# Retention's squares and roots moved by a round, one-column sums in another form, and norm-weight scaling moved by a supertile, in a two-layer encoder trunk

## The chip, the cores and the metric

One core of one Trainium2 chip runs the kernel. The metric is device time in microseconds (us) from the start to the end of one execution. The kernel before the change was timed three times: 2040.69, 2045.63 and 2047.82 us, median 2045.63 us. A further execution was profiled.

## What is computed

Two layers act on x, 2048 tokens of 1024 columns, and a final RMSNorm ends the work:

```
hn   = rms_norm(x, norm_gain)
proj = hn @ w_in                      # 1024 -> 8 sections of 512 columns
ya   = chunked_rel_attention(aq, ak, av, rel_bias)   # 8 heads x 64, own chunk and 8 left
yr   = rms_norm(o_intra + o_inter)    # 4 retention heads x 128, chunkwise recurrent
x    = x + concat(ya * silu(ag), yr * silu(rg)) @ w_out
```

In the retention part, o_intra multiplies decayed scores (q times k, times a decay mask) with v; o_inter multiplies q with a running state; the state is scaled and added to, chunk after chunk. The sum o is divided, per row and head, by the root of its mean square.

## The kernel before

**Number format.** Each projection and most other products are made of three float16 matmuls: a value is split in an upper half and the rest (upper times upper, upper times rest, rest times upper). The ScalarE (ACT) usually writes the upper half by a copy; the VectorE (DVE) then writes the rest.

**Loops.** Layer l has four column groups s (two attention heads and one retention head each), and each group runs over four supertiles n of 512 tokens. For each (l, s, n), `dense_T` computes q, k and the rotary q and k (line 763: 4 x 24 matmuls of 128x512), and `dense_V` computes the two v and the two gates (line 783: 4 x 24). While these run, the attention and retention of the *previous* supertile run between their matmuls. After the four groups, `wout` (line 1161) multiplies with w_out and adds to x, row tile by row tile; the last group's attention and retention run beside its first rounds. In the first layer the second layer's input norm and first weights are prepared beside it as well.

**Rounds.** Everything goes by rounds. `run` advances the dense generator by one step (8 matmuls of 128x512), calls `tick`, which issues what was put off with `later(k, fn)` and is due in this round, in the order in which it was put off, then advances the attention by one step, and last pulls steps of the background list `bg` (weights of the next group, `prep_T`, `prep_V`, `prep_Omax`, `prep_O`). A supertile has 12 rounds of `dense_T` and 12 of `dense_V`.

**Order of the queues.** TensorE (PE), ACT, DVE and GpSimd (POOL) stand under a manual schedule: each executes its instructions in the order in which the Python code issues them. An instruction that waits holds all behind it on its engine. SyncE (SP) issues the DMAs; its order is made by a planner from the program, save for DMAs that `in_turn` keeps in program order.

**An attention unit** (one head, 128 queries, three rounds): scores S on PE (lines 831, 832); bias and row maximum on DVE (L835, L837); the exponential on ACT (L838) and its float16 copy (L840); the rest on POOL (L841); a DMA transposes both (L843, tile pT); three rounds later PE multiplies with v (L853, L854).

**A retention tile** (128 tokens, tile a of the supertile):

| round | instructions |
|---|---|
| 6a | scores r1 on PE (L888) |
| 6a+1 | decay mask, DVE L907 |
| 6a+2 | upper half dT, ACT L892 |
| 6a+3 | rest of dT, DVE L896 |
| 6a+5 | output and state products r2, PE L888; the last of the output's six products reads the rest of dT |
| +1 | state addition, DVE L928 |
| +2 | upper half of the state (sh), ACT L892; square of the output with a row sum into ss, ACT L949 |
| +3 | rest of the state, DVE L896; `root`: mean and epsilon on DVE L940, power -1/2 on POOL L941 |
| +4 | `fin`: output times root times gate, DVE L945; its store goes out a round later (L947) |
| +5 | state times the chunk decay, ACT L936 |

The rounds marked +k count from the round of r2. The next tile's round 6a+6 is +1, so its mask (L907) is issued at +2, its upper half at +3 and its rest (L896, dT) at +4, where `fin` of the tile before stands ahead of it.

**One-column work.** Each weight section is scaled by a power of two. `sumsq` squares it on ACT (L320) with a row sum, `lowp` casts the column (L327), `allsum` sums over the rows by a matmul with ones (L334), and `norm_scale` makes the scales on DVE (L151 to L155). `prep_Omax` does the same for w_out over eight blocks and adds their columns one by one (L522); its matmul (msO) follows four rounds after the last addition, and six one-column instructions (L336 to L531) follow that. `gain_scale(1)` does a like chain for the second layer's norm weights in three parts; it is started at (l, s, n) = (0, 1, 1), beside `prep_T` of the next group.

Of the kernel before, what the change touches and what calls it, by code (L numbers as in the profile page):

```python
# [10 lines left out]
F32 = mybir.dt.float32  # L11
I32 = mybir.dt.int32
AF = mybir.ActivationFunctionType
ALU = mybir.AluOpType
# [4 lines left out]
P = 128  # L19
# [8 lines left out]
def hybrid_trunk(ctx: ExitStack, tc: tile.TileContext, x, pos, gain, gcol, w_in, w_out, rel, fgain,  # L28
# [8 lines left out]
    act, dve, pool, pe, sp = nc.scalar, nc.vector, nc.gpsimd, nc.tensor, nc.sync  # L37
# [24 lines left out]
    mhalf = cp.tile([P, 1], F32, tag="mhalf", name="mhalf")  # L62
# [83 lines left out]
    def norm_scale(sq, nm, ig=None, k=14):  # L146

        e = b2.tile([P, 1], I32, tag="p2e", name=f"e{nm}")
        s = b2.tile([P, 1], I32, tag="p2s", name=f"s{nm}", bufs=8)
        i = b2.tile([P, 1], I32, tag="p2i", name=f"i{nm}", bufs=12)  # L150
        dve.tensor_scalar(e, sq.bitcast(I32), 24, 23, op0=ALU.logical_shift_right, op1=ALU.logical_shift_left)  # L151
        dve.tensor_scalar(s, e, -1.0, float((190 + k) << 23), op0=ALU.mult, op1=ALU.add)
        dve.tensor_scalar(i, e, float((64 - k) << 23), None, op0=ALU.add)
        if ig is not None:
            dve.tensor_tensor(i.bitcast(F32), i.bitcast(F32), ig, op=ALU.mult)  # L155
        return s.bitcast(F32), i.bitcast(F32)

    gains = {}
# [249 lines left out]
    def V_units(l, s, g, iv, nm):  # L408

        g.urv = mul_cols("urv", dcs[:, s:s + 1], None, 2.0 ** -11, nm)  # L410
        g.ugh = mul_cols("ugh", iv[2], None, 2.0 ** -11, nm)
        g.ka = mul_cols("ka", iv[0], iv[2], 2.0 ** -5, nm)
        gk = mul_cols("gqk", iv[2], dcs[:, 4 + s:5 + s], 2.0 ** -11, nm)
        g.re = mul_cols("re", iv[1], g.qk, 2.0 ** (31 + s), nm)
        act.activation(g.re, g.re, AF.Copy, scale=gk[:, 0:1])
        yield
        for u in (gk, g.re):
            dve.tensor_tensor(u, u, u, op=ALU.mult)
            dve.reciprocal(u, u)
        dve.tensor_scalar(g.re, g.re, EPS, 2.0 ** -120, op0=ALU.mult, op1=ALU.max)  # L420
        dve.tensor_scalar(g.re, g.re, 2.0 ** 120, None, op0=ALU.min)
        g.ra = mul_cols("ra", gk, dcs[:, 8 + s:9 + s], 1.0, nm)
        yield

    def prep_V(l, s, g):
        nm = f"V{l}_{s}"
        g.vh = b3.tile([P, KT, 512], F16, tag="wh", name=f"wh{nm}")
        g.vl = b3.tile([P, KT, 512], F16, tag="wl", name=f"wl{nm}")
        c0 = s * P
        sts = []  # L430

        def ld(j):
            o = VSEC[j] * 512 + c0
            sts.append(load_sec(w_in[l, :, o:o + P], f"{nm}{j}"))

        def sq(j):
            return sumsq(sts[j], f"{nm}{j}", g.vh[:, :, j * P:(j + 1) * P])

        def cv(j, s_):
            return convert(sts[j], g.vh[:, :, j * P:(j + 1) * P], g.vl[:, :, j * P:(j + 1) * P], s_)  # L440

        def rest(k):
            for _ in range(k):
                yield

        ld(0)
        ld(1)
        yield
        iv = [None] * 3
        m1 = [None] * 2  # L450
        for j in range(2):
            yield
            m1[j] = lowp(sq(j), f"{nm}{j}")
            yield from rest(3)
            m = allsum(m1[j], f"{nm}{j}")
            sv, iv[j] = norm_scale(m, f"{nm}{j}", gains[l].i)
            yield from cv(j, sv)
            ld(2 + j)
        yield from rest(1)
        m2 = sq(2)  # L460
        yield
        yield from rest(1)
        m3 = sq(3)
        dve.tensor_tensor(m2, m2, m3, op=ALU.add)
        m2 = lowp(m2, f"{nm}2")
        yield
        yield from rest(2)
        m = allsum(m2, f"{nm}2")
        sv, iv[2] = norm_scale(m, f"{nm}2", gains[l].i)
        for _ in V_units(l, s, g, iv, nm):  # L470
            pass
        yield from cv(2, sv)
        yield from cv(3, sv)
        g.vdone = 4

    def prep_V_next(l, g):

        nm = f"V{l}_0"
        src = [w_in[l, :, VSEC[j] * 512:VSEC[j] * 512 + P] for j in range(4)]
        sts = [load_sec(src[j], f"{nm}{j}", True) for j in range(2)]  # L480
        yield
        for j in (2, 3):
            st = b2.tile([P, KT, P], F32, tag="q", name=f"st{nm}{j}")
            sp.dma_start(st, src[j].rearrange("(k p) c -> p k c", p=P))
            sts.append([(st, 0, KT)])
        yield
        g.vh = b3.tile([P, KT, 512], F16, tag="wh", name=f"wh{nm}")
        g.vl = b3.tile([P, KT, 512], F16, tag="wl", name=f"wl{nm}")
        hi, lo = ([w_[:, :, j * P:(j + 1) * P] for j in range(4)] for w_ in (g.vh, g.vl))
        m = [lowp(sumsq(sts[j], f"{nm}{j}", hi[j]), f"{nm}{j}") for j in range(2)]  # L490
        yield
        m2, m3 = (sumsq(sts[j], f"{nm}{j}", hi[j]) for j in (2, 3))
        dve.tensor_tensor(m2, m2, m3, op=ALU.add)
        m.append(lowp(m2, f"{nm}2"))
        yield
        yield
        iv = [None] * 3
        for j in (2, 0, 1):
            sv, iv[j] = norm_scale(allsum(m[j], f"{nm}{j}"), f"{nm}{j}", gains[l].i)
            for i in ((2, 3) if j == 2 else (j,)):  # L500
                yield from convert(sts[i], hi[i], lo[i], sv)
        yield from V_units(l, 0, g, iv, nm)
        g.vdone = 4

    def prep_Omax(l, go):
        nm = f"O{l}"
        mm = b2.tile([P, 1], F32, tag="omax", name=f"omax{nm}")
        load = lambda j: load_sec(w_out[l, :, j * P:(j + 1) * P], f"{nm}m{j}")
        for _ in range(4):
            yield  # L510
        sts = [load(0), load(1)]
        for _ in range(4):
            yield
        for j in range(KT):
            yield
            m1 = sumsq(sts[j], f"{nm}m{j}", None)
            if j + 2 < KT:
                sts.append(load(j + 2))
            if j == 0:
                dve.tensor_copy(mm, m1)  # L520
            else:
                dve.tensor_tensor(mm, mm, m1, op=ALU.add)  # L522
        mm = lowp(mm, nm)
        for _ in range(4):
            yield
        m = allsum(mm, nm)
        sv, iv = norm_scale(m, nm)
        go.os = b2.tile([P, 1], F32, tag="o_s", name=f"o_s{l}")
        go.oi = b2.tile([P, 1], F32, tag="o_i", name=f"o_i{l}")
        dve.tensor_copy(go.os, sv)  # L530
        dve.tensor_copy(go.oi, iv)  # L531
        yield
# [87 lines left out]
    def later(k, fn):  # L620
        deferred.append([k, fn])
# [276 lines left out]
    def retention(l, s, n, g, st):  # L898
        for a in range(4):
# [18 lines left out]
            if not last:  # L918
# [4 lines left out]
                ns = ring["state"]  # L923
# [9 lines left out]
                later(1, add)  # L933
                later(2, lambda sh=sh, ns=ns: upper_of(sh, ns))
                later(3, lambda sh=sh, ns=ns: rest_of(sh, ns))
                later(5, lambda ns=ns: act.activation(ns, ns, AF.Copy, scale=(1.0 - 2.0 ** (-5 - s)) ** P))  # L936
            ss = b2.tile([P, 1], F32, tag="rss", name=f"rss{nm}")

            def root(ss=ss):
                dve.tensor_scalar(ss, ss, g.ra[:, 0:1], g.re[:, 0:1], op0=ALU.mult, op1=ALU.add)  # L940
                pool.tensor_tensor(ss, ss, mhalf, op=ALU.pow)  # L941

            def fin(t=t, a=a, r2=r2, ss=ss, nm=nm):
                y = b1.tile([P, P], F32, tag="yr", name=f"yr{nm}")
# [1 line left out]
                                         op0=ALU.mult, op1=ALU.mult)  # L946
                later(1, lambda: in_turn(sp.dma_start(y_d[t][:, 512 + s * P:512 + (s + 1) * P], y)))  # L947

            later(2, lambda r2=r2, ss=ss: act.activation(r2[:, 2 * P:3 * P], r2[:, 0:P], AF.Square,  # L949
                                                         accum_out=ss))  # L950
            later(3, root)
            later(4, fin)
            yield


# [32 lines left out]
    def y_scale(u, go):  # L988
        dve.tensor_scalar(u.m, u.m, 2.0 ** -100, None, op0=ALU.max)
        u.sy, iy = norm_scale(u.m, u.nm)  # L990
        u.sc = b2.tile([P, 1], F32, tag="osc", name=f"osc{u.nm}", bufs=4)
        dve.tensor_tensor(u.sc, iy, go.oi, op=ALU.mult)

    def y_turn(u):
        if u.t + 1 == NT:
# [262 lines left out]
    def weight_steps():  # L1258
# [20 lines left out]
        def vsq(j):  # L1279
            m[j] = sumsq(sts[j], f"{nm}{j}", g.vh[:, :, j * P:(j + 1) * P])  # L1280
            if j == 3:
                dve.tensor_tensor(m[2], m[2], m[3], op=ALU.add)
            if j != 2:
                m[j] = lowp(m[min(j, 2)], f"{nm}{j}")

# [186 lines left out]
    for l in range(DEPTH):  # L1472
        gO = [Grp(), Grp()]
        go = Grp()
        for s in range(NSW):
            g = grp(l, s)
            for n in range(NS):
# [12 lines left out]
                if (l, s) == (0, 0) and 0 < n < NS - 1:  # L1490
# [3 lines left out]
                    if n == 2:  # L1494
                        t3 = tables((3,), [xs0[3][:, i * 256:(i + 1) * 256] for i in range(4)])
                        steps["v"] = lambda: go_on(t3)
                if (l, s, n) == (0, 1, 1):
                    for l_ in range(1, DEPTH):
                        gr = gain_scale(l_)
                        later(2, lambda gr=gr: next(gr))  # L1500
                        later(10, lambda gr=gr: next(gr))
                        later(18, lambda gr=gr: next(gr))
# [113 lines left out]
```

## Time and profile before

| | |
|---|---|
| median of three runs | 2045.63 us |
| the profiled execution, its own time | 2046.1 us |
| its span, first to last instruction | 2044.0 us |
| mean granted TensorE clock | 0.995 |
| PE, DVE, ACT, POOL busy | 1992.2, 1249.5, 1136.1, 694.1 us |
| DMA | 313.47 MB, 153 GB/s on average |

The span and the execution's own time differ by 2.1 us, which lies around the instructions. Engines overlap, so that their busy times don't add up. A line of the view of waits names the instruction that sat waiting, what released it, the total in us, how often and the longest. In the timeline a row has its start in us from the span's start, its duration in us, engine, line, operation and tiles, and in brackets the idle time of the engine ahead of it with the releaser.

### The profile page before, as it was taken

How to read it: one execution, taken by the hardware profiler on the slowest of the kernel's cores; microseconds unless marked ns; L12 is line 12 of the kernel's file. 1: busy time of each engine (PE TensorE's matmuls, PEld its weight loads, DVE VectorE, ACT ScalarE, POOL GpSimd, SP SyncE). 2: the span in 40 equal slices, each digit the busy share in tenths (PEclk: the TensorE clock that was granted, in tenths of full speed). 3: DMA queues.
4: the chain of work that ended last, by engine and by line, in shares of the span. 5: the costliest groups of instructions: out<-in, count | busy, mean ns of one | idle time of the engine just before them, and what ended most of it. 6: DMA issues, size and time to landing. Idle time of an engine off the chain costs nothing. (4 is left out here: it accounts for less than half of the span.)

```text
span 2044.0 us, 36842 instructions
## 1 busy us (share of the span) xinstructions
PE 1992.2 (97%) x12918; PEld 1047.1 (51%) x12918; DVE 1249.5 (61%) x3676; ACT 1136.1 (56%) x2526; POOL 694.1 (34%) x701
## 2 busy tenths in 40 slices
PE   7998999999999999999999999999999999999998
PEld 5444554555545555554444555555555555555444
DVE  7687766565666555676553656565656566557543
ACT  7565765465565654655444546655656565455432
POOL 1344433443334434430003433444343434343100
PEclk9999999999999999999999999999999999999999
DMA  8787775456575654899774647454656766558874
GB/s 234 180 180 161 162 147 116 107 129 146 118 177 126 162 131 101 170 215 262 216 188 110 129 100 162 113 130 99 160 120 146 156 156 127 123 120 187 227 204 136
DMA packets 645690, 313.47 MB, mean 153 GB/s; under 512 B 459232, under 2 KB 602080, under 8 KB 645504
## 3 DMA queue, kind: packets, MB, share of 16 engines
q1 hardware_dynamic: 645504, 311.12, 65.3%
q8 instruction: 101, 1.65, 0.3%
q14 instruction: 85, 0.70, 0.1%
HBM read 123.26 MB, written 41.98 MB: 81 GB/s over the span
## 5 line engine op out<-in xcount | busy, mean ns | idle before, releaser
L841 POOL TENSOR_TENSOR pq<-sc,pq 128x640 f16<-128x640 f32 (+4 forms) x256 | 322.0, 1258 | 857.6 <-ACT pq L840 460.5
L838 ACT ACTIVATE sc<-sc,mq,cT 128x640 f32<-128x640 f32 (+4 forms) x256 | 218.4, 853 | 597.0 <-DVE mq L837 432.3
L783 PE MATMUL dV<-whV,hTh 128*128 128x512 f16 x1024 | 352.0, 379 | 1.3 <-DVE gt L801 1.3
L763 PE MATMUL dT<-hTh,whT 128*128 128x512 f16 x1008 | 348.5, 381 | 4.0 <-DVE xa L94 3.9
L783 PE MATMUL dV<-wlV,hTh 128*128 128x512 f16 x1024 | 352.0, 379 | 0.0
L783 PE MATMUL dV<-whV,hTl 128*128 128x512 f16 x1024 | 351.8, 379 | 0.0
L763 PE MATMUL dT<-hTh,wlT 128*128 128x512 f16 x1008 | 347.8, 380 | 0.0
L763 PE MATMUL dT<-hTl,whT 128*128 128x512 f16 x1008 | 346.9, 379 | 0.0
L783 PEld LDWEIGHTS <-hTh 128*128 128x128 f16 x2048 | 196.3, 98 | 214.8 <-DVE gt L801 2.7
L763 PEld LDWEIGHTS <-whT 128*128 128x128 f16 x2016 | 192.6, 98 | 210.6 <-DVE xa L94 4.4
L835 DVE CUSTOM_DVE_ANT_0 sc<-S,bias 128x640 f32<-128x640 f32 (+4 forms) x256 | 188.4, 736 | 91.6 <-PE S L832 89.6
L1161 PE MATMUL dO<-whO,yhy 128*128 128x512 f16 x504 | 191.8, 381 | 1.8 <-DMA yhy<-hTh 1.8
L1161 PE MATMUL dO<-whO,yly 128*128 128x512 f16 x504 | 191.7, 380 | 0.3 <-DMA yly<-hTh 0.3
L1161 PE MATMUL dO<-wlO,yhy 128*128 128x512 f16 x504 | 191.6, 380 | 0.0
L840 ACT ACTIVATE pq<-sc 128x640 f16<-128x640 f32 (+4 forms) x256 | 171.5, 670 | 8.1
L1161 PEld LDWEIGHTS <-yhy 128*128 128x128 f16 x1008 | 98.3, 98 | 115.5 <-DMA yhy<-hTh 2.3
L783 PEld LDWEIGHTS <-hTl 128*128 128x128 f16 x1024 | 99.1, 98 | 111.7 <-issue 2.1
L763 PEld LDWEIGHTS <-wlT 128*128 128x128 f16 x1008 | 97.7, 98 | 108.8 <-issue 1.5
L853 PE MATMUL o<-v,pT 128*128 128x129 f16 x1120 | 133.1, 222 | 14.7 <-DMA pT<-pq 14.6
L831 PE MATMUL S<-k,q 128*128 128x128 f16 (+3 forms) x592 | 143.1, 268 | 0.0
L832 PE MATMUL S<-k,q 128*128 128x128 f16 (+3 forms) x592 | 130.0, 268 | 0.0
L853 PEld LDWEIGHTS <-pT 128*128 128x128 f16 x1120 | 103.5, 98 | 50.7 <-DMA pT<-pq 22.6
(360 smaller groups left out, 3283.3 us busy)
## 6 DMA issues: line engine op xcount, KB each, us to landing
q<-qq SPq DMA_DIRECT2D x128, 128.0 KB, 2.4
yyy<-y_d SPq DMA_DIRECT2D x32, 512.0 KB, 4.5
stT<-in_w_in_dram SPq DMA_DIRECT2D x27, 512.0 KB, 4.9
stV<-in_w_in_dram SPq DMA_DIRECT2D x26, 512.0 KB, 4.5
k<-kk SPq DMA_DIRECT2D x128, 64.0 KB, 2.0
swp<-rot SPq DMA_DIRECT2D x64, 128.0 KB, 3.0
tabc<-tab SPq DMA_DIRECT2D x32, 256.0 KB, 2.9
tabs<-tab SPq DMA_DIRECT2D x32, 256.0 KB, 3.1
```

Of the source, the lines that this page charges most:

```text
L763: pe.matmul(ps, w_[:, j, kt, :], h_[:, kt, :], start=(m == 0), stop=(m == 23))
L783: pe.matmul(ps, h_[:, kt, a * P:(a + 1) * P], w_[:, kt, :], start=(m == 0), stop=(m == 23))
L831: pe.matmul(o, st.q[:, hx, 0, cs], k_, start=True, stop=False)
L832: pe.matmul(o, st.q[:, hx, 1, cs], k_, start=False, stop=True)
L835: dve.tensor_tensor_reduce(out=v, in0=S[:, 0:w], in1=g.bias[hx][:, 640 - w:640], scale=1.0, scalar=-3.0e38, op0=ALU.add, op1=ALU.max, accu ...
L838: act.activation(v, v, AF.Exp, bias=m[:, 0:1], scale=g.c[:, 0:1])
L840: act.activation(pq[:, 0:w], v, AF.Copy)
L841: pool.tensor_tensor(pq[:, w:2 * w], v, pq[:, 0:w], op=ALU.subtract)
L853: pe.matmul(o[:, u.hx, 0:129], u.p[:, b, :], v_, start=(b == 0), stop=False)
L1161: pe.matmul(ps, h_[:, kt, :], w_[:, kt, :], start=(m == 0), stop=(m == 23))
```

## The change

- Retention: the square is issued at +1 instead of +2, the root at +2 instead of +3, the state's decay at +4 instead of +5. `fin` is still due at +4, but it is put off from inside `root`, so that it is now issued behind the next tile's rest of dT of that round.
- Seven places of one-column products and sums on DVE change from tensor_tensor to tensor_scalar with the second column as a per-row scalar.
- `prep_Omax` waits five rounds instead of four ahead of its matmul.
- `gain_scale(1)` starts at (0, 1, 2) instead of (0, 1, 1).

```diff
-            dve.tensor_tensor(i.bitcast(F32), i.bitcast(F32), ig, op=ALU.mult)
+            dve.tensor_scalar(i.bitcast(F32), i.bitcast(F32), ig[:, 0:1], None, op0=ALU.mult)
...
-            dve.tensor_tensor(u, u, u, op=ALU.mult)
+            dve.tensor_scalar(u, u, u[:, 0:1], None, op0=ALU.mult)
...
-        dve.tensor_tensor(m2, m2, m3, op=ALU.add)
+        dve.tensor_scalar(m2, m2, 1.0, m3[:, 0:1], op0=ALU.mult, op1=ALU.add)
...
-                dve.tensor_tensor(mm, mm, m1, op=ALU.add)
+                dve.tensor_scalar(mm, mm, 1.0, m1[:, 0:1], op0=ALU.mult, op1=ALU.add)
         mm = lowp(mm, nm)
-        for _ in range(4):
+        for _ in range(5):
             yield
...
-                later(5, lambda ns=ns: act.activation(ns, ns, AF.Copy, scale=(1.0 - 2.0 ** (-5 - s)) ** P))
+                later(4, lambda ns=ns: act.activation(ns, ns, AF.Copy, scale=(1.0 - 2.0 ** (-5 - s)) ** P))
...
+            def root(ss=ss, fin=fin):
+                dve.tensor_scalar(ss, ss, g.ra[:, 0:1], g.re[:, 0:1], op0=ALU.mult, op1=ALU.add)
+                pool.tensor_tensor(ss, ss, mhalf, op=ALU.pow)
+                later(2, fin)
+
-            later(2, lambda r2=r2, ss=ss: act.activation(r2[:, 2 * P:3 * P], r2[:, 0:P], AF.Square,
+            later(1, lambda r2=r2, ss=ss: act.activation(r2[:, 2 * P:3 * P], r2[:, 0:P], AF.Square,
                                                          accum_out=ss))
-            later(3, root)
-            later(4, fin)
+            later(2, root)
...
-        dve.tensor_tensor(u.sc, iy, go.oi, op=ALU.mult)
+        dve.tensor_scalar(u.sc, iy, go.oi[:, 0:1], None, op0=ALU.mult)
...
-                if (l, s, n) == (0, 1, 1):
+                if (l, s, n) == (0, 1, 2):
                     for l_ in range(1, DEPTH):
                         gr = gain_scale(l_)
```

The additions in `prep_V_next` and in `vsq` change like the one in `prep_V` that is shown. In the built programs PE's matmuls keep their order except for four one-column ones (msg, msh and the two msO), which move later. On SP ten or so of the DMAs change places with a neighbour, mostly a pT transpose that now stands ahead of a store or of the transpose of rotary k. On POOL the root's power keeps its place among the exponentials' rests (L841) but for the first of all; it moves ahead of the bias memsets (L597, L598) in six places and ahead of the row norms' powers (L219) in eight.

More of the change, by code (lines that the diff above doesn't have):

```diff
@@ L492, in prep_V_next @@
         m2, m3 = (sumsq(sts[j], f"{nm}{j}", hi[j]) for j in (2, 3))
-        dve.tensor_tensor(m2, m2, m3, op=ALU.add)
+        dve.tensor_scalar(m2, m2, 1.0, m3[:, 0:1], op0=ALU.mult, op1=ALU.add)
         m.append(lowp(m2, f"{nm}2"))
@@ L935, in retention @@
                 later(3, lambda sh=sh, ns=ns: rest_of(sh, ns))
-                later(5, lambda ns=ns: act.activation(ns, ns, AF.Copy, scale=(1.0 - 2.0 ** (-5 - s)) ** P))
+                later(4, lambda ns=ns: act.activation(ns, ns, AF.Copy, scale=(1.0 - 2.0 ** (-5 - s)) ** P))
             ss = b2.tile([P, 1], F32, tag="rss", name=f"rss{nm}")
-            def root(ss=ss):
-                dve.tensor_scalar(ss, ss, g.ra[:, 0:1], g.re[:, 0:1], op0=ALU.mult, op1=ALU.add)
-                pool.tensor_tensor(ss, ss, mhalf, op=ALU.pow)
             def fin(t=t, a=a, r2=r2, ss=ss, nm=nm):
@@ L1281, in vsq @@
             if j == 3:
-                dve.tensor_tensor(m[2], m[2], m[3], op=ALU.add)
+                dve.tensor_scalar(m[2], m[2], 1.0, m[3][:, 0:1], op0=ALU.mult, op1=ALU.add)
             if j != 2:
```

## The prediction

> **What bounds the kernel now.** I read the page's busy times first, then what PE waited for.
>
> ```profile
> PE 1992.2 (97%) x12918; PEld 1047.1 (51%) x12918; DVE 1249.5 (61%) x3676; ACT 1136.1 (56%) x2526; POOL 694.1 (34%) x701
> ```
>
> PE works for 1992.2 of the span's 2044.0 us and the change leaves its work as it is. Only the 51.8 us without a matmul can shrink, and a new wait on another engine costs nothing until PE meets it. So the view of waits, for PE alone, is the ledger (line waited, releaser, total us, times, longest):
>
> ```profile
> PE o L853 <- DMA pT<-pq: 14.6, 12, 2.7
> PE r L888 <- DVE dT L896: 6.5, 7, 1.6
> PE dO L1161 <- DMA yhy<-hTh: 1.8, 1, 1.8
> PE dV L783 <- DVE gt L801: 1.3, 2, 0.7
> PE msT L334 <- DVE mbT L327: 1.2, 1, 1.2
> PE msO L334 <- DVE mbO L327: 0.2, 1, 0.2
> ```
>
> The first line, DMA transposes of the softmax, is the largest, and no edit acts on it directly. The lines released by DVE, 9.2 us together, are an in-order engine being late, and the change works on its queue and on those that feed it. The timeline of PE gives their places (start, duration, idle ahead):
>
> ```profile
> 339.42 0.16 PE L334 MATMUL msT<-mbT,ones 128*128 128x1 bf16 x1 [1.23 <-DVE mbT L327]
> ...
> 586.98 0.23 PE L888 MATMUL r<-rv,dT 128*128 128x128 f16 x1 [1.32 <-DVE dT L896]
> ...
> 594.64 0.39 PE L783 MATMUL dV<-whV,hTh 128*128 128x512 f16 x1 [0.64 <-DVE gt L801]
> ...
> 601.99 0.23 PE L888 MATMUL r<-rv,dT 128*128 128x128 f16 x1 [0.67 <-DVE dT L896]
> ...
> 860.01 0.23 PE L888 MATMUL r<-rv,dT 128*128 128x128 f16 x1 [1.60 <-DVE dT L896]
> 862.96 0.23 PE L853 MATMUL o<-v,pT 128*128 128x129 f16 x1 [0.83 <-DMA pT<-pq]
> ...
> 1594.51 0.39 PE L783 MATMUL dV<-whV,hTh 128*128 128x512 f16 x1 [0.66 <-DVE gt L801]
> ...
> 1601.85 0.23 PE L888 MATMUL r<-rv,dT 128*128 128x128 f16 x1 [0.67 <-DVE dT L896]
> ```
>
> So the waits stand where one-column chains run: beside the norm weights (339), the w_out sums of both layers (587 to 602, and 1594, 1602), and where w_out is multiplied first (860). Elsewhere DVE and ACT are late without PE noticing.
>
> **The change, part by part.**
>
> *Norm weights one supertile on.* The timeline of DVE ahead of 339:
>
> ```profile
> 329.56 0.15 DVE L336 TENSOR_SCALAR m2h<-msh 128x1 f32<-128x1 f32 x1
> ...
> 332.02 0.15 DVE L196 SCALAR_TENSOR_TENSOR ge<-gi 128x1 f32<-128x1 f32 x1
> ...
> 339.21 0.16 DVE L327 CAST mbT<-m1T 128x1 bf16<-128x1 f32 x1 [3.44 <-ACT whT L320]
> ```
>
> The norm-weight chain holds DVE from 329.56 to 332.17, 2.6 us. Behind it come the row maximum, the exponential that waits for it, and only then on ACT the weight square that feeds mbT. With the chain gone all of these come up to 2.6 us sooner, more than the 1.23 us that PE waits: **-1.2 us**. The chain now runs in the next supertile (two windows, one a supertile: length, busy times PE, PEld, DVE, ACT, POOL):
>
> ```profile
> 313.00:365.00 52.00, 50.60 (x329) 26.09 (x327) 35.85 (x121) 28.97 (x71) 19.69 (x19) 1.00 0.52 114
> 365.00:417.00 52.00, 52.00 (x366) 28.26 (x365) 28.42 (x85) 25.19 (x59) 20.95 (x19) 1.00 0.50 116
> ```
>
> There PE never idles and DVE has 23.6 us free of 52, because no weights are prepared. I cost the chain at nothing there; without that cover it would cost its 2.6 us once, since the row maximum and the gate's rest, which free PSUM, queue behind it.
>
> *The w_out sums: tensor_scalar, and a round more.* The timeline of DVE around 587 to 602:
>
> ```profile
> 586.29 0.16 DVE L522 TENSOR_TENSOR omaxO<-omaxO,m1O0m 128x1 f32<-128x1 f32 x1 [0.44 <-ACT stO0m L320]
> 586.38 0.35 DVE L945 SCALAR_TENSOR_TENSOR yr<-r,rss,gt 128x128 f32<-128x128 f32 x1
> 586.65 0.28 DVE L896 SCALAR_TENSOR_TENSOR dT<-dT,r 128x128 f16<-128x128 f16 x1
> ...
> 592.47 1.12 DVE L522 TENSOR_TENSOR omaxO<-omaxO,m1O0m 128x1 f32<-128x1 f32 x1
> ...
> 600.67 0.15 DVE L336 TENSOR_SCALAR m2O<-msO 128x1 f32<-128x1 f32 x1
> ...
> 601.38 0.35 DVE L945 SCALAR_TENSOR_TENSOR yr<-r,rss,gt 128x128 f32<-128x128 f32 x1
> 601.65 0.28 DVE L896 SCALAR_TENSOR_TENSOR dT<-dT,r 128x128 f16<-128x128 f16 x1
> ```
>
> One sum of one column takes 0.16 us or 1.12 us. The view by line gives the spread (min/median/max in ns), beside forms that use per-row scalars already:
>
> ```profile
> L155 DVE TENSOR_TENSOR iT<-iT,gi x28: 159/161/1326, 199.5 to 1549.8; 128x1 f32<-128x1 f32 x28
> L992 DVE TENSOR_TENSOR oscy<-iy,o_i x32: 158/160/162, 816.9 to 2014.0; 128x1 f32<-128x1 f32 x32
> L837 DVE TENSOR_SCALAR mq<-mq,ncT x256: 211/214/217, 73.6 to 1909.3; 128x1 f32<-128x1 f32 x128
> L940 DVE TENSOR_SCALAR rss<-rss,raV,reV x128: 258/262/273, 100.5 to 1918.5; 128x1 f32<-128x1 f32 x128
> ```
>
> Undisturbed, a per-row scalar costs 214 - 160 = 54 ns more; but 384 such instructions never went over 273 ns beside a busy POOL, where tensor_tensor reached 1326. I take 214 ns. The added 54 ns on the 32 instructions of L992, 1.7 us, lies on DVE beside w_out's matmuls; uncovered it would cost that. The other places (L155 and the like, one or two a weight section) are shorter on balance and stand where PE has no wait, so I cost them at nothing; by their undisturbed price they would add 54 ns each.
>
> The Trainium skill, page "SBUF — State Buffer", section "Who interferes with whom", says that a DVE instruction with two SBUF inputs contends with GpSimd's reads, which agrees with the spread. It also says that tensor_scalar can enter modes that hold the shared pair of ports, which speaks against the edit: by it the new form could stall as the old one did. L837 and L940 speak against that here.
>
> At 592.47 the shorter sum gives back 1.12 - 0.21 = 0.9 us: the 0.64 us of the gate's wait behind it goes, with msO's wait of 0.2 (in the waits above it is the second layer's; I leave out the first layer's). At 601.65 the six instructions from 600.67 to 601.38, 0.7 us, go behind the rest of dT, with fin: 1.0 us for a wait of 0.67. The added round issues msO later on PE; nothing reads its result until w_out is split in the next group. Both layers: 0.64 + 0.67 and 0.2 + 0.66 + 0.67, **-2.8 us**.
>
> *Output behind the rest of dT.* At 586.38 fin stands ahead of the rest of dT by 0.27 us (586.65 - 586.38); what is late next is ACT's w_out square, which L522 waits for. **-0.3 us**. At 860 and in the second layer it is the same 0.27 us, but the pT wait follows 2.95 us later and follows a DMA, so I count that as given back: 0 to -0.5.
>
> *Squares, roots and decay a round sooner.* Instructions and their durations (views by line):
>
> ```profile
> L949 ACT ACTIVATE r<-r 128x128 f32<-128x128 f32 x128 | 32.9, 257 | 0.0
> L949 ACT ACTIVATION_READ_ACCUMULATOR r<-r 128x1 f32 x128 | 23.2, 181 | 0.0
> L936 ACT ACTIVATE state<-state 128x128 f32<-128x128 f32 x120 | 35.1, 293 | 0.0
> L941 POOL TENSOR_TENSOR rss<-rss,mhalf 128x1 f32<-128x1 f32 x128 | 76.6, 599 | 136.5 <-DVE rss L940 129.6 <-ACT rot L695 6.8
> L838 ACT ACTIVATE sc<-sc,mq,cT 128x640 f32<-128x640 f32 (+4 forms) x256 | 218.4, 853 | 597.0 <-DVE mq L837 432.3 <-DVE rl L862 98.8 <-DVE ymy L989 20.1
> ```
>
> And the view of waits has DVE waiting for the power:
>
> ```profile
> DVE yr L945 <- POOL rss L941: 21.7, 35, 0.7
> ```
>
> The square with its sum, 0.26 + 0.18 = 0.44 us, now stands ahead of an exponential, in ACT's idle time: 597.0 / 256 = 2.3 us on average. POOL's 129.6 us of idling for the root shrinks, so that rotary work behind it starts sooner, and DVE's 21.7 us of waiting for the power should go: the root keeps a round of lead. DVE's root waits for a square issued a round before it; behind it on DVE stand the next mask and the rest of the state, which PE reads four rounds later. ACT's decay now waits for that rest with an exponential behind it, but this exponential waits for a row maximum that DVE issues later still. What this gives PE I can bound only: between nothing and the share of the DMA waits that hang on a late softmax rest (14.6 us of pT and 1.8 of yhy). The longest such saving on one chain is 0.7 us, DVE's longest wait for the power; three of these would be 2 us. I take **-0.7 us**, one such step, as DVE's waits are near PE's in few places. SP's queue keeps its work; the transposes that move up pass a store or a transpose.
>
> **Sum:** -1.2 - 2.8 - 0.3 - 0.7 = **-5.0 us** against the profiled execution's 2046.1 us (its span and 2.1 us around it): 2041.1 us, or 2040.6 against the runs' median of 2045.63. I forecast **2041 us**.
>
> **The rivals.**
>
> 1. *Given back.* The time saved ends in the next DMA wait, as at 862.96. For it: pT is PE's largest wait. Against it: no wait is listed between 345 and 585 or 602 and 857. If most goes so, about 1 us is left: **2045 us**.
>
> 2. *More than the sum: the clock.* The windows with their granted clock (after the busy times):
>
> ```profile
> 119.20:122.60 3.40, 3.40 (x14) 1.47 (x15) 3.33 (x14) 1.75 (x7) 0.55 (x1) 0.50 0.98 193
> ...
> 931.50:934.90 3.40, 3.40 (x10) 1.24 (x9) 3.33 (x6) 1.43 (x2) 0.00 (x0) 0.50 1.08 296
> ```
>
> Three waits (the other at 194) were followed by 3.4 us at half clock, which loses 1.7 us each. If sooner roots shorten those waits so that two stretches go, -5 - 3.4 - 1 of the waits themselves: **2036.5 us**. The Trainium skill, "TensorE: Matmul & The Clock Gate", section "Part 1: The HAM clock gate", explains such stretches by free-running windows of activity; so they may also come or go by phase alone.
>
> 3. *Slower: the square ahead of the exponential.* If ACT is not idle there, each late exponential delays its pT by 0.44 us. It decides where PE already waits for pT, which the view of L853 counts, weight loads included:
>
> ```profile
>   DMA pT<-pq: 37.3, 30
> ```
>
> Thirty places at 0.44 us are 13.2 us; less the 5.0 gained, **+8 us, 2054 us**. It needs ACT's idle time ahead of L838 to be under 0.44 us there; the mean of 2.3 us speaks against it.
>
> 4. *The edit of the sums does nothing*, if the new form is held up like the old at 592.47: the waits for gt and msO stay, 1.3 + 0.2 us, and the time is 2042.6 us.
>
> **How the numbers follow.** Forecast 0.47, given back 0.2, more 0.2, slower 0.07, the sums held up 0.06. A measurement of this kernel tells about 0.3%, 6.1 us, from no change: the three runs lie 7.1 us apart. Under 2039.5 us lie the third case and a quarter of the forecast's own spread of 3 us either way: 0.32 faster. Over 2051.8 us lies rival 3 and little else: 0.08 slower. 0.60 is within. The range 2036 to 2047 takes in all cases but the slower one and part of the third, with the spread of the runs.
>
> **What would show it.** In the profile after: no wait of msT beside 339 and none in the next supertile; no wait of dV for gt and of r near 602 and 1602; L522 at most 0.28 us; DVE's wait for the power near zero; the r wait at 587 still there, by 0.3 us smaller. It is wrong if PE's pT total rises by what the other waits lose, or if PE waits for anything behind L949 or L940.

## The result, and the profile after

Over 17 runs each, the kernel before had a median of 2043.38 us and the changed kernel 2034.96 us (2032.27 to 2041.86). The ratio is **0.9965**, 95% interval [0.9955, 0.9975]: 0.35% faster, some 7.2 us of 2045.63 (5.1 to 9.2), where 5.0 were forecast and a change within 0.3% was taken as the likeliest. By the ratio the time is 2038.5 us, inside the range; the median itself lies 1 us below its lower end. The ratio is not the quotient of the two medians, which is 0.9959; for the experiments below, too, the ratio with its interval decides, and the medians are given beside it. The profiled execution of after had a span of 2033.0 us, 11.0 less than before's.

The first part of the page of after, with the busy times:

```profile
PE 1988.2 (98%) x12918; PEld 1046.3 (51%) x12918; DVE 1241.9 (61%) x3676; ACT 1154.5 (57%) x2526; POOL 705.8 (35%) x701
```

PE is idle for 44.8 us instead of 51.8 us: 7.0 of the 11.0 us are waits that went. The rest is time of the same matmuls, which the prediction took as fixed; of that, 1.7 us are a stretch at half clock (below), and 2.3 I can't place. The waits of PE in after, the same view and columns as of before:

```profile
PE o L853 <- DMA pT<-pq: 15.0, 9, 3.1
...
PE r L888 <- DVE dT L896: 3.0, 4, 1.1
...
PE dO L1161 <- DMA yhy<-hTh: 1.1, 1, 1.1
PE dV L783 <- DVE gt L801: 1.1, 2, 0.5
```

The lines for msT and msO are gone, r lost 3.5 us and yhy 0.7, the gate lost 0.2 and pT gained 0.4. What is left of the listed places, in the timeline of PE:

```profile
581.86 0.23 PE L888 MATMUL r<-rv,dT 128*128 128x128 f16 x1 [0.69 <-DVE dT L896]
...
589.12 0.39 PE L783 MATMUL dV<-whV,hTh 128*128 128x512 f16 x1 [0.53 <-DVE gt L801]
...
852.28 0.23 PE L888 MATMUL r<-rv,dT 128*128 128x128 f16 x1 [0.67 <-DVE dT L896]
...
855.89 0.23 PE L853 MATMUL o<-v,pT 128*128 128x129 f16 x1 [1.49 <-DMA pT<-pq]
...
1584.03 0.39 PE L783 MATMUL dV<-whV,hTh 128*128 128x512 f16 x1 [0.53 <-DVE gt L801]
```

Before's r waits at 602 and 1602 have no row here. The gate's waits, forecast to go, are still 0.53 us each; at 852 (860 before) 0.93 us of the r wait went, and the pT wait behind it grew by 0.66. The exponential and the power, in the view by line (busy, mean ns, idle time ahead), and DVE's wait for the power:

```profile
L838 ACT ACTIVATE sc<-sc,mq,cT 128x640 f32<-128x640 f32 (+4 forms) x256 | 218.3, 853 | 416.0 <-DVE mq L837 294.2 <-DVE rl L862 86.9 <-DVE ymy L989 16.9
L947 POOL TENSOR_TENSOR rss<-rss,mhalf 128x1 f32<-128x1 f32 x128 | 93.7, 732 | 16.9 <-DVE rss L946 14.9 <-DVE ssf L217 2.1
```

```profile
DVE yr L941 <- POOL rss L947: 3.6, 14, 0.4
```

ACT's idle time ahead of the exponential fell from 597.0 to 416.0 us (109.6 us of it now stand ahead of the square), POOL's ahead of the power from 136.5 to 16.9, and DVE waits 3.6 us for the power where it waited 21.7. Which of these three PE felt, the profile can't say. The experiments had to.

### The profile page after: what moved, and what is told of

Read it like the earlier page. It is cut to its first block, busy times and chain, and to the rows that moved or that the text cites. A ratio compares the mean times of both kernels' runs of the same rounds, so it can differ in the third digit from the quotient of the medians.

```text
span 2033.0 us, 36844 instructions
## 1 busy us (share of the span) xinstructions
PE 1988.2 (98%) x12918; PEld 1046.3 (51%) x12918; DVE 1241.9 (61%) x3676; ACT 1154.5 (57%) x2526; POOL 705.8 (35%) x701
## 4 chain that ended last, share of the span: by engine, by line
PE 86%; DMA 4%; DVE 3%; ACT 2%; POOL 2%; issue 2%; SPq 1%; POOLq 0%; ACTq 0%; DVEq 0%
PE dT L763 29%; PE dV L783 27%; PE dO L1161 15%; PE r L888 4%; PE o L853 3%; PE S L832 3%; PE S L831 3%; DMA pT<-pq 2%; PE o L854 2%; POOL swp L704 0%; PE dT L745 0%; DVE sc L835 0%; DMA xa<-in_x_dram 0%; DMA swp<-rot 0%; ACT stO0m L320 0%
## 5 line engine op out<-in xcount | busy, mean ns | idle before, releaser
L841 POOL TENSOR_TENSOR pq<-sc,pq 128x640 f16<-128x640 f32 (+4 forms) x256 | 322.8, 1261 | 958.0 <-ACT pq L840 497.4
L838 ACT ACTIVATE sc<-sc,mq,cT 128x640 f32<-128x640 f32 (+4 forms) x256 | 218.3, 853 | 416.0 <-DVE mq L837 294.2
L763 PE MATMUL dT<-hTh,whT 128*128 128x512 f16 x1008 | 348.3, 381 | 3.1 <-DMA hTh<-hTl 3.1
L763 PE MATMUL dT<-hTh,wlT 128*128 128x512 f16 x1008 | 348.1, 381 | 0.0
L763 PE MATMUL dT<-hTl,whT 128*128 128x512 f16 x1008 | 346.6, 379 | 0.0
L763 PEld LDWEIGHTS <-whT 128*128 128x128 f16 x2016 | 192.4, 98 | 209.3 <-DVE xb L98 3.6
L763 PEld LDWEIGHTS <-wlT 128*128 128x128 f16 x1008 | 97.7, 98 | 109.1 <-issue 2.1
```

What stands on the lines that cost most here:

```text
L763: pe.matmul(ps, w_[:, j, kt, :], h_[:, kt, :], start=(m == 0), stop=(m == 23))
L838: act.activation(v, v, AF.Exp, bias=m[:, 0:1], scale=g.c[:, 0:1])
L841: pool.tensor_tensor(pq[:, w:2 * w], v, pq[:, 0:w], op=ALU.subtract)
```

## The experiments

Each kernel is timed against the kernel before on the same chip.

**The parts one by one.** Four kernels on one chip, before's median 2045.4 us over 35 runs. `ret_only` is before with the retention's lines alone:

```diff
-                later(5, lambda ns=ns: act.activation(ns, ns, AF.Copy, scale=(1.0 - 2.0 ** (-5 - s)) ** P))
+                later(4, lambda ns=ns: act.activation(ns, ns, AF.Copy, scale=(1.0 - 2.0 ** (-5 - s)) ** P))
...
+            def root(ss=ss, fin=fin):
...
+                later(2, fin)
...
-            later(2, lambda r2=r2, ss=ss: act.activation(r2[:, 2 * P:3 * P], r2[:, 0:P], AF.Square,
+            later(1, lambda r2=r2, ss=ss: act.activation(r2[:, 2 * P:3 * P], r2[:, 0:P], AF.Square,
                                                          accum_out=ss))
-            later(3, root)
-            later(4, fin)
+            later(2, root)
```

> Only the retention part of the change: square, root and decay a round sooner, output behind the next rest of dT. Theory of the queues (each part removes the waits that its own DVE and ACT instructions caused): the waits at 585 and 587 fall from 0.51 and 1.32 us to about 0.7 together, those at 602 and 1602 from 0.67 to about 0.4, the one at 860 from 1.60 to 0.7 with half of that given back at the next pT wait, while msT at 339 (1.23) and dV at 594 and 1594 (0.64, 0.66) stay; 3 to 4 us less in all, of which the sum of the prediction had 1.0. Rival, clock: what the changed kernel gained beyond 5 us is the half-clock stretch that is missing near 931, so that this kernel gains about 1 us when it keeps that stretch and about 2.7 when it doesn't, and its waits between 580 and 870 are as before but for 0.3 us.

`rest_only` is after without these lines.

> The change without its retention part: per-row scalars, the fifth round of the w_out sums, norm weights a supertile later. Theory of the queues: msT at 339 gone, dV at 594 and 1594 down from 0.65 us to at most 0.5, r at 602 and 1602 gone, msO gone; the waits at 585, 587, 860 and 1859 as before; 4 us less. Rival, clock: the same 4 us or more, as the retention part is worth 1 us at most.

`gain_only` moves the norm weights alone:

```diff
-                if (l, s, n) == (0, 1, 1):
+                if (l, s, n) == (0, 1, 2):
```

> Only the norm weights' scaling one supertile on. Theory of the queues: the waits at 339 and 341 (1.23 and 0.12 us) go, nothing appears between 365 and 417, all other waits of TensorE stay in size; 1.4 us less. Rival, given back: the next pT at 356 becomes a wait of 1 us and nothing is gained.

`wsum_only` has the per-row scalar in L522 and the fifth round:

```diff
-                dve.tensor_tensor(mm, mm, m1, op=ALU.add)
+                dve.tensor_scalar(mm, mm, 1.0, m1[:, 0:1], op0=ALU.mult, op1=ALU.add)
...
-        for _ in range(4):
+        for _ in range(5):
```

> Only the w_out sums: L522 with a per-row scalar, and the fifth round ahead of their matmul. Theory of the queues: L522 at 0.21 to 0.28 us each time, dV at 594 and 1594 gone or at most 0.5 us, r at 602 and 1602 gone, msO gone, 587 as before; 2 to 2.8 us less. Rival, ports (the new form is held up like the old): L522 up to over 1 us, dV waits of 0.65 us stay, only the 0.67 us of r go, 1.5 us less.

| kernel | median us | ratio, 95% | of 2045 us |
|---|---|---|---|
| ret_only | 2040.03 | 0.9976 [0.9966, 0.9987] | -4.9 |
| rest_only | 2041.87 | 0.9982 [0.9971, 0.9993] | -3.7 |
| gain_only | 2044.17 | 0.9997 [0.9988, 1.0006] | -0.6 |
| wsum_only | 2042.55 | 0.9990 [0.9979, 1.0001] | -2.0 |

0.9976 times 0.9982 is 0.9958, within after's interval: within the intervals the parts add up. The retention part, which I had valued at 1.0 us (0.7 and 0.3), is the largest. It also acts where the norm weights act: the timeline of PE in `ret_only` has

```profile
336.60 0.16 PE L334 MATMUL msT<-mbT,ones 128*128 128x1 bf16 x1 [0.27 <-DVE mbT L327]
```

so 0.96 of the 1.23 us went without moving the norm weights. Beside 585 and 587 less went than expected: the two waits are 0.69 and 0.97 us there, where 0.7 together was expected.

**Which line of the retention part.** Three kernels and one for the sums on one chip, before's median 2045.19 us over 33 runs. `root_sooner`: square at +1, root at +2, `fin` and decay as before.

> Before, with the square and the root one round sooner; the output keeps its round and its place ahead of the rest of dT, the decay too. Theory A (lead of the root): DVE's wait for the power falls from 21.7 us to under 2, the ratio is 0.9975 to 0.9985, and most of the retention part's 4.9 us is here. Theory B (place of the output): the wait for the power falls all the same, but PE's r waits at 587, 860 and 1859 stay above 1.2 us each, and the ratio is 0.9995 to 1.001.

`fin_behind`: `fin` alone goes behind the next rest of dT, still at +4.

```diff
                 pool.tensor_tensor(ss, ss, mhalf, op=ALU.pow)
+                later(1, lambda: fin())
...
             later(3, root)
-            later(4, fin)
```

> Before, with the output step alone put behind the next rest of dT; square, root and decay keep their rounds. The retention part as a whole measured a ratio of 0.9976, some 4.9 us. Theory A (the part gains because the root has more lead, so that DVE no longer waits for the power): here DVE's wait for the power stays near 20 us, the r waits at 587, 860 and 1859 fall by 0.27 us each at most, and the ratio is 0.9995 to 1.000. Theory B (the part gains because the output no longer stands ahead of the rest of dT on DVE): the r waits lose 0.27 us and also the wait for the power that stood ahead of the output, so that those of before 860 and 1859 fall to about 0.5, and the ratio is 0.998 to 0.999.

`decay_only`: `later(5, ...)` of the decay becomes `later(4, ...)`.

> Before, with the decay of the state alone one round sooner. Theories A and B both leave nothing for it: ratio 0.9995 to 1.0005, PE's waits within 0.3 us of before's each, apart from the half-clock stretches. Theory C (ACT is freed where the exponentials stand): PE's wait for pT falls by 1 us or more and the ratio is 0.999 or less.

| kernel | median us | ratio, 95% | DVE's wait for the power | PE's r waits for dT | pT |
|---|---|---|---|---|---|
| root_sooner | 2042.73 | 0.9985 [0.9975, 0.9996] | 7.1 | 3.9 | 15.1 |
| fin_behind | 2044.08 | 0.9996 [0.9986, 1.0006] | 13.1 | 5.0 | 16.1 |
| decay_only | 2044.22 | 0.9992 [0.9983, 1.0002] | 21.7 | 6.4 | 16.9 |

In `fin_behind` the r waits are 1.5 us smaller and pT is 1.5 larger (14.6 to 16.1). Two executions of after differ by as much in pT (15.0 and 16.5), so that the profile can't show that the time was given back; in time the output's place can't be told from nothing, and neither can the decay. The square and the root carry most of the gain, 3.1 us (0.8 to 5.1), as theory A expected, though 7.1 us of the wait for the power stay where it had under 2.

**Square or root?** Reading the trace of `root_sooner` gave a theory D: not the root's lead counts, but that the square leaves its place *behind* the exponential. The timeline of ACT in before, ahead of the msT wait:

```profile
335.66 0.81 ACT L838 ACTIVATE sc<-sc,mq,cT 128x512 f32<-128x512 f32 x1 [4.14 <-DVE mq L837]
336.50 0.63 ACT L840 ACTIVATE pq<-sc 128x512 f16<-128x512 f32 x1
337.04 0.61 ACT L708 ACTIVATE rot<-raw 128x512 f16<-128x512 f32 x1
337.56 0.29 ACT L892 ACTIVATE sh<-state 128x128 f16<-128x128 f32 x1
337.76 0.26 ACT L949 ACTIVATE r<-r 128x128 f32<-128x128 f32 x1
337.95 0.18 ACT L949 ACTIVATION_READ_ACCUMULATOR r<-r 128x1 f32 x1
338.04 1.04 ACT L320 ACTIVATE whT<-stT 128x1024 f16<-128x1024 f32 x1
```

ACT idles 4.14 us ahead of the exponential and then has a row of work without a gap, with the square in it and the weight square, for which mbT and msT wait, right behind. `square_sooner` moves the square alone; the power keeps its round:

```diff
-            later(2, lambda r2=r2, ss=ss: act.activation(r2[:, 2 * P:3 * P], r2[:, 0:P], AF.Square,
+            later(1, lambda r2=r2, ss=ss: act.activation(r2[:, 2 * P:3 * P], r2[:, 0:P], AF.Square,
                                                          accum_out=ss))
             later(3, root)
             later(4, fin)
```

> Before, with the retention's square alone one round sooner; the root, the output and the decay keep their rounds. Theory A (lead of the root: DVE no longer waits for the power): the power is issued in the same round as before, so DVE's wait for it stays near 21 us, PE's waits for msT, r and gt stay as before, and the ratio is 0.9995 to 1.0005. Theory D (ACT's queue: the 0.44 us of the square go into the idle time ahead of the exponential, so that what stood behind them on ACT, the weight squares and the reads of dV, comes 0.44 us sooner): the wait for the power stays near 21 us too, but ACT's idle time ahead of the exponential falls from 597 to about 455 us, the msT wait of 1.2 us goes, PE's idle time falls by 2 to 4 us, and the ratio is 0.998 to 0.999.

Measured: 2043.20 us, ratio **0.9983** [0.9973, 0.9994], before 2044.86 over 15 runs. ACT's timeline at the same place:

```profile
335.95 0.26 ACT L949 ACTIVATE r<-r 128x128 f32<-128x128 f32 x1 [3.23 <-DVE state L928]
336.13 0.20 ACT L949 ACTIVATION_READ_ACCUMULATOR r<-r 128x1 f32 x1
336.87 0.81 ACT L838 ACTIVATE sc<-sc,mq,cT 128x512 f32<-128x512 f32 x1 [0.55 <-DVE mq L837]
...
338.77 0.29 ACT L892 ACTIVATE sh<-state 128x128 f16<-128x128 f32 x1
338.97 1.04 ACT L320 ACTIVATE whT<-stT 128x1024 f16<-128x1024 f32 x1
```

From the exponential's start to the weight square's it is now 338.97 - 336.87 = 2.10 us, before 338.04 - 335.66 = 2.38: the 0.28 us that the square took of ACT's queue there (337.76 to 338.04) are gone. Over the whole run ACT's idle time ahead of the exponential is 462.5 us, near the 455 of theory D. DVE's wait for the power has not changed:

```profile
DVE yr L945 <- POOL rss L941: 21.6, 35, 0.7
```

and PE's waits are 0.18 us for msT (1.23 before) and, of the r waits, 0.62 at 859 (1.60 at 860 before) in its timeline:

```profile
340.35 0.16 PE L334 MATMUL msT<-mbT,ones 128*128 128x1 bf16 x1 [0.18 <-DVE mbT L327]
...
587.54 0.23 PE L888 MATMUL r<-rv,dT 128*128 128x128 f16 x1 [1.25 <-DVE dT L896]
...
859.42 0.23 PE L888 MATMUL r<-rv,dT 128*128 128x128 f16 x1 [0.62 <-DVE dT L896]
```

Theory A is not borne out: with the whole wait for the power left in place, the ratio is that of `root_sooner`, as far as the intervals tell (1.2 to 5.5 us here; the medians lie only 1.7 us apart). The places speak against it too. Of the 35 waits for the power in before, none stands in the 16 us ahead of a listed wait of PE for DVE or ACT; the last one ahead of 587 is

```profile
568.25 0.35 DVE L945 SCALAR_TENSOR_TENSOR yr<-r,rss,gt 128x128 f32<-128x128 f32 x1 [0.66 <-POOL rss L941]
```

D holds at msT, at 859 and in its ratio, but not at the gate, whose waits are still 1.3 us, and not in its sum: PE's idle time in this profile was to fall by 2 to 4 us and rose by 2.0, from 51.8 to 53.8. This execution was the slowest of its 11 (2046.48 us; the fastest 2036.67), and the largest new wait, 1.64 us for dT at 1586, has another source. It is released through the sum of L522 by a weight square, for which ACT sat waiting for a DMA (0.24 us at the same place in `root_sooner`):

```profile
1584.83 1.06 ACT L320 ACTIVATE stO1m<-stO1m 128x1024 f32<-128x1024 f32 x1 [1.68 <-DMA stO1m<-in_w_out_dram]
```

The root's move seems to have an effect of its own, too. PE's r waits for dT are 1.9 to 3.9 us in the six profiles that have the root a round sooner and 5.0 to 7.8 in the eight others, with `square_sooner` at 7.8 the largest. One place shows a way that needs no wait for the power. From DVE's rest of the rotary values (L711) to the rest of dT, ahead of PE's r wait of 0.67 us at 602, `square_sooner` has

```profile
598.66 1.47 DVE L711 TENSOR_TENSOR rot<-raw,rot 128x512 f16<-128x512 f32 x1 [2.13 <-ACT rot L708]
...
600.26 0.26 DVE L940 TENSOR_SCALAR rss<-rss,raV,reV 128x1 f32<-128x1 f32 x1
...
602.20 0.28 DVE L896 SCALAR_TENSOR_TENSOR dT<-dT,r 128x128 f16<-128x128 f16 x1
```

and `root_sooner`

```profile
596.43 1.47 DVE L711 TENSOR_TENSOR rot<-raw,rot 128x512 f16<-128x512 f32 x1 [1.95 <-ACT rot L708]
...
599.79 0.28 DVE L896 SCALAR_TENSOR_TENSOR dT<-dT,r 128x128 f16<-128x128 f16 x1
```

That is 602.20 - 598.66 = 3.54 us, as in before (601.65 - 598.11), and 599.79 - 596.43 = 3.36: the root's DVE instruction, L940, has left this row, and the r wait behind it is gone. So the same may hold on DVE's queue for the root as on ACT's for the square. How the 3 us divide between the two, neither the intervals nor these profiles settle.

D has a second consequence: more work ahead of the exponential should cost nothing. `extra_ahead` is after with two more squares of the same scores at each of the 128 places; their results are not read:

```diff
+            for _ in range(2):
+                later(1, lambda r2=r2: act.activation(r2[:, 3 * P:4 * P], r2[:, 0:P], AF.Square))
             later(2, root)
```

> After, with two more squares of the same scores (128x128 each, some 0.4 us together, into columns that nothing reads) issued on ACT right behind the retention's square, so ahead of the exponential: 128 such places, 51 us more work for ACT. Theory D (what counts is ACT's work behind the exponential; ahead of it ACT is idle): ACT's idle time ahead of the exponential falls from 416 to some 365 us or less, PE's waits for r and gt stay within 0.5 us of after's, and the ratio to before stays 0.9955 to 0.9975. Rival (ACT's work as such is what PE waits for, wherever it stands): the 3 to 4 us that moving the square gained go again, and the ratio is 0.998 to 0.999.

Measured: 2036.36 us, before 2046.27 over 9 runs, ratio 0.9956 [0.9942, 0.9969], that of after. Its view by line:

```profile
L838 ACT ACTIVATE sc<-sc,mq,cT 128x640 f32<-128x640 f32 (+4 forms) x256 | 218.3, 853 | 348.4 <-DVE mq L837 236.3 <-DVE rl L862 86.2 <-DVE ymy L991 15.7
...
L953 ACT ACTIVATE r<-r 128x128 f32<-128x128 f32 x256 | 67.1, 262 | 8.1
```

The added work is 67.1 us; the idle time ahead of the exponential fell by as much (416.0 to 348.4), and the time shows no loss, within an interval of some 2.7 us either way. That rules out ACT's work as such, wherever it stands, for which 0.998 to 0.999 was expected.

**The sums.** `form_only`, with the second set, changes L522's form and leaves four rounds.

> Before, with the running sum of the w_out squares alone in the per-row scalar form, still four rounds ahead of msO. If the stretched sum at 592 is what makes the gate late, the new sum takes 0.21 us and the gate's wait falls from 0.64 to about 0.47, where ACT's output of rv, with two weight squares ahead of it, is late next, and no further; both layers together 0.4 us of PE at most, a ratio of 0.9995 to 1.000. If the new form is held up as the old was, the sum at 592 takes about 1 us again and the gate's wait stays at 0.64. The r waits at 602 and 1602 stay 0.67 in either case, as the fifth round is not there.

Measured: 2046.06 us, ratio 0.9995 [0.9986, 1.0004]. The timeline of PE in `form_only`, and then in `wsum_only`, where the row for r is missing:

```profile
596.06 0.39 PE L783 MATMUL dV<-whV,hTh 128*128 128x512 f16 x1 [0.47 <-DVE gt L801]
603.40 0.23 PE L888 MATMUL r<-rv,dT 128*128 128x128 f16 x1 [0.67 <-DVE dT L896]
```

```profile
595.68 0.39 PE L783 MATMUL dV<-whV,hTh 128*128 128x512 f16 x1 [0.47 <-DVE gt L801]
```

So the form takes 0.17 us from the gate's wait and the fifth round takes the 0.67 us of r. What holds the gate is in the timelines of ACT and then DVE in after:

```profile
584.68 1.04 ACT L320 ACTIVATE stO0m<-stO0m 128x1024 f32<-128x1024 f32 x1
...
586.24 1.04 ACT L320 ACTIVATE stO0m<-stO0m 128x1024 f32<-128x1024 f32 x1
...
587.28 0.26 ACT L791 ACTIVATE v<-dV 128x128 f16<-128x128 f32 x1
```

```profile
588.19 0.29 DVE L797 SCALAR_TENSOR_TENSOR v<-dV,v 128x128 f16<-128x128 f32 x1 [0.38 <-ACT rv L793]
```

Two weight squares stand ahead of ACT's reads of dV, and DVE, which writes the gate behind L797, sits waiting for the last of these reads. `sums_behind` is after with the last of the squares a round later, each sum a round later, and the length that the background list is told one step more:

```diff
             yield
+            if j == KT - 1:
+                yield
             m1 = sumsq(sts[j], f"{nm}m{j}", None)
...
-                dve.tensor_scalar(mm, mm, 1.0, m1[:, 0:1], op0=ALU.mult, op1=ALU.add)
+                later(1, lambda m1=m1: dve.tensor_scalar(mm, mm, 1.0, m1[:, 0:1], op0=ALU.mult, op1=ALU.add))
...
-        mm = lowp(mm, nm)
-        for _ in range(5):
+        yield
+        mm_ = lowp(mm, nm)
+        for _ in range(4):
             yield
...
-                    push(prep_Omax(l, go), 21)
+                    push(prep_Omax(l, go), 22)
```

> After, with each running sum of the w_out squares put one round later, behind the rest of dT, and the last square one round later, behind ACT's reads of dV; the conversion of the sum follows a round later. If ACT's weight squares are what is still late beside 582 and 589 and in the second layer, the r wait of 0.69 falls to under 0.1, the gt waits of 0.53 to under 0.2, and the time is 1 to 1.7 us below that of after: a ratio of 0.9955 to 0.996 to before. If the time is given back at the transposes of the softmax, PE's wait for pT rises from 15.0 to over 16 us and the ratio is that of after, 0.9965.

`after_again` is after once more beside it.

> After, unchanged, for a second profile and for the comparison on one chip: ratio 0.9955 to 0.9975. If the stretches at half clock belong to the program, they start at 119.4 and 184.2 us again and none stands between 190 and 2000 us; if they go by a phase that differs from one execution to the next, one or two start elsewhere or are added, with the same waits of PE ahead of them.

`sums_behind`: 2035.16 us, ratio 0.9954 [0.9942, 0.9967]; `after_again`: 2036.62 us, 0.9959 [0.9947, 0.9972]. In the waits of PE the gate's line is gone and dT's is smaller:

```profile
PE o L856 <- DMA pT<-pq: 15.3, 11, 2.6
...
PE r L891 <- DVE dT L899: 1.9, 4, 0.7
...
PE r L891 <- ACT dT L895: 0.7, 1, 0.7
PE r L891 <- DVE sh L899: 0.6, 1, 0.6
```

The gate's waits went as expected; as the squares and the sums were moved together, the run doesn't say which of the two it was. Beside 582 a wait of 0.7 us for ACT's copy of dT stands in place of the one for the rest of dT; `after_again`, where the sums are as in after, has one of 0.6. The 1.5 us between the medians can't be told from no difference; it is at least no worse than after.

**The clock.** The windows of after at the places of its own stretches and of before's third one (length, PE, PEld, DVE, ACT, POOL busy, granted clock, DMA share, GB/s), then `after_again` at its own and at after's:

```profile
119.40:122.80 3.40, 3.40 (x10) 1.20 (x9) 3.26 (x15) 1.62 (x4) 0.55 (x1) 0.50 0.94 183
184.20:187.60 3.40, 2.81 (x19) 1.94 (x20) 0.82 (x2) 0.37 (x2) 0.00 (x0) 0.50 0.45 104
931.50:934.90 3.40, 3.40 (x18) 1.41 (x16) 2.87 (x9) 1.52 (x4) 0.00 (x0) 1.00 1.06 264
```

```profile
111.60:115.00 3.40, 3.40 (x20) 2.04 (x17) 3.25 (x2) 1.06 (x1) 3.37 (x2) 0.50 0.44 96
119.40:122.80 3.40, 3.13 (x20) 1.53 (x20) 3.13 (x13) 1.62 (x5) 0.55 (x1) 1.00 1.02 209
184.20:187.60 3.40, 3.03 (x26) 1.81 (x27) 1.05 (x3) 0.66 (x1) 0.00 (x0) 1.00 0.47 111
193.50:196.90 3.40, 2.96 (x17) 1.77 (x18) 0.83 (x2) 0.00 (x0) 0.00 (x0) 0.50 1.07 240
```

The same program has its stretches elsewhere in its next execution. Before's third stretch, at 931, is missing from after and just as well from `gain_only`, `wsum_only` and `form_only`, which change little or nothing near there: the 1.7 us it cost belong to that execution, not to the change. That agrees with the Trainium skill, "TensorE: Matmul & The Clock Gate", "Part 1: The HAM clock gate", by which the windows run freely and the same kernel meets them at another phase from run to run.

## Why the prediction was right or wrong

- **Norm weights, -1.2.** The wait at 339 went and none came in the next supertile. Alone the edit measured 0.6 us, with nothing inside its interval. Beside the retention part it has little left to take, as that part alone leaves 0.27 us of this wait.
- **The w_out sums, -2.8.** Measured 2.0; the interval holds 2.8 and, barely, nothing. That the fifth round takes the 0.67 us at 602 and 1602 was right. The step that failed is "the 0.64 us of the gate's wait behind it goes": it fell to 0.53. I freed DVE and did not ask what else the gate waits for: ACT's rv, behind two weight squares, was late as well, and DVE still sits 0.38 us waiting for it.
- **L522 and the per-row scalar.** L522 now takes 203 to 215 ns in all 14 places, where it took up to 1222. Rival 4 is out. What the Trainium skill's page "SBUF — State Buffer", "Who interferes with whom", says against the form, modes that hold the shared ports where the operands meet their conditions, shows in none of these rows.
- **Output behind the rest of dT, -0.3, given back at 860.** Not contradicted: `fin_behind` alone measured 0.8 us with nothing inside its interval. In after, a pT wait that is larger by 0.66 us follows the 0.93 us that went at 860, as was taken.
- **Squares, roots and decay a round sooner, -0.7.** This term was the miss, and with it the sum. The retention part measured 4.9 us (2.7 to 7.0) where it stood with 1.0; of that, square and root together measured 3.1, and the square alone 3.5 (1.2 to 5.5). The working had the right fact, that the square "now stands ahead of an exponential, in ACT's idle time", and used it only to show that nothing is lost. It then followed the root to DVE's wait for the power, which fell as forecast, but `square_sooner` has most of the gain in time without that, and no listed wait of PE for DVE follows one of these closely. The step that was not taken is to list what stood *behind* the old places: behind the square on ACT weight squares, reads of dV and copies of dT, behind L940 on DVE reads of dV and the rest of dT. The square kept them back by 0.28 us and L940 by 0.18 where they are measured above, and each stands at 128 places. That places like these make up the whole 4.9 us is argued, not shown.
- **The rivals.** *Given back*: not seen as a whole; PE's pT total rose by 0.4 us beside the 7.0 that its idle time lost, and two executions of after differ by 1.5 in it. *Slower*: in `extra_ahead` three squares ahead of the exponential cost nothing that the time shows. *The clock*: a stretch less in the profiled pair, for no cause in the change that these runs show. Whether after meets fewer stretches on the whole stays open: before's mean clock over 92 runs is 0.9963, after's over 22 is 0.9969, and 0.0006 of 2040 us would be 1.2 us of the gain.
- **What would show it.** DVE's wait for the power fell to 3.6 us, near what was said, and it did not matter. The r wait at 587 is still there, as said; it fell by 0.63 in after and by 0.29 in `after_again` (1.03 us), where 0.3 was said.

Not settled is how the retention's 4.9 us divide. The root was never moved alone; the output and the decay alone are each within their interval of nothing; and PE's waits point at square and root together more than at the square.

## What to carry to other kernels

On an engine that executes in order, idle time has a place. An instruction moved from behind the engine's long wait to ahead of it can free its time for everything that was queued behind it (0.28 us of ACT's at 338, 0.18 of DVE's at 602), and here it cost nothing that showed where it now stands; so list both queues, the one it leaves and the one it joins. And where a wait on one engine is removed, look up the second latest input of the same consumer before the whole wait is put down as a gain.

## What was not expected of the hardware

The sum of two one-column operands on DVE took anything from 151 to 1222 ns (L522 of before) while one-column work with a per-row scalar never left 203 to 216 ns, in L522 and in the 49 products of L155:

```profile
L155 DVE TENSOR_SCALAR iT<-iT,gi x28: 213/214/216, 198.4 to 1538.8; 128x1 f32<-128x1 f32 x28
L522 DVE TENSOR_SCALAR omaxO<-omaxO,m1O0m x7: 204/214/215, 569.8 to 587.4; 128x1 f32<-128x1 f32 x7
```

Two of the long sums of before, read in the timelines, end with an instruction of POOL that was already running. The one of 1.12 us runs from 592.47 to 593.59, and beside it POOL has, until 593.57,

```profile
592.31 1.26 POOL L704 TENSOR_TENSOR swp<-swp,tabs 128x512 f32<-128x512 f32 x1
```

The one of 0.42 us at 590.71 ends at 591.13, POOL's L841 beside it at 591.12.

Runs of one and the same program differ by up to 10 us (2036.67 to 2046.48 for `square_sooner`). Part of it goes with the clock: in before's 35 runs of the first set the mean granted clock went from 0.993 (2048.8 us) to 0.999 (2040.8 us). Part lies at the start: in the two profiles of after the first matmuls of L763 that wait for hTh begin at 68.99 and 71.14 us, and of the 2.4 us between the two spans only 0.2 are left behind that point. POOL's power took 732 ns on average where it stands a round sooner and 599 ns in before; the profiles don't say why.
